# Out-projection weights in a hybrid decoder layer: load and split written as two pieces, each behind the softmax of a named attention step

## The chip, the cores and the metric

The kernel runs on one core of a Trainium2 chip. The metric is the time of one launch in microseconds (us) of the device, lower is better. Five engines work side by side: TensorE (PE in the profile, PEld for its weight loads), VectorE (DVE), ScalarE (ACT), GpSimd (POOL) and SyncE (SP), whose queue issues most of the DMA transfers. The built program holds one list of instructions for each engine; an instruction that waits holds back those that stand behind it in its list.

## The reference, cut to what matters

One decoder layer on 1024 tokens of width 1024, float32:

```
h = RMSNorm(x);  z = h @ W_in                      # one projection, columns split
A = dilated sliding-window attention(q, k, v)      # 8 heads x 64, then RMSNorm with attn_out_gain
R = RWKV-7 time mixing(z)                          # 8 heads x 64
x = x + RMSNorm(concat[A, R] @ W_out)              # W_out: 1024 x 1024
x = x + RMSNorm(relu(RMSNorm(x) @ W_up)^2 @ W_down)
```

The change concerns the preparation of `W_out`. The three branches of the attention are computed as one dense causal attention with a bias table (`stripT`), so that each softmax row is one exponential over its keys.

## The kernel before, in words

All large products are done as three products of rounded parts (`mm3`, lines 49 to 67): an operand `a` is split into a rounded `hi` and the rest `lo`, and `hi*hi + lo*hi + hi*lo` is summed in PSUM. So every weight block has to be split before TensorE can use it: ScalarE writes `hi`, VectorE subtracts it from the raw block and writes `lo`.

The program has these stages in time: input norm and transposes; a long stage in which the columns of `z` are projected slab by slab while the RWKV units are woven in (`drive`, up to about 447 us in the profiled execution); the attention (about 455 to 600 us); the out-projection with its norms ("mix", up to about 690 us); the up-projection and the down-projection of the feed-forward part.

**The attention** is written as 64 steps `m`. Step `m` stands for a pair of heads `p = m // 16`, a block of 128 queries `i` (in the order `TO` = 0, 4, 1, 5, 2, 6, 3, 7) and one head `h` of the pair; steps 1 and 2 are swapped. A step has these parts:

- `at_s`: TensorE forms the scores `pS` (two products per bank of 512 keys, 128*(i+1) keys in all) in PSUM banks of the tags `w` and `z`; VectorE adds the bias and takes the minimum (line 927, one instruction per bank, then a short read of the accumulator); ScalarE takes the exponential over the row (line 929).
- `at_t`: TensorE transposes the exponentials in blocks of 128 (`pT`, line 939) into the banks `a` and `c`, which exist once each; ScalarE copies the first four blocks out (line 941), VectorE the others (line 943).
- `at_v`: TensorE multiplies with the values (`po`); `at_vt` turns the values of the next pair (`vt`, again banks `a` and `c`).

The scores of step `m + 2` are written ahead of the transposes of step `m`, so TensorE runs two steps ahead of the softmax. The last slab of the projection, `z_av`, is woven into the start: its first half (24 products) and three parts of three products of its second half stand ahead of the first scores (`LEAD = 11` parts), and one part of three in each of the next steps. `z_av` uses the two banks `z`; its second half needs the bank that the eviction of the second half of `z_ak` frees (`evh_ak` on ScalarE, line 722, and `evl_ak` on VectorE, line 723).

**The out-projection weights** are eight blocks `k` of 128 x 1024. `load_wo(k)` (line 974) issues the load into a raw buffer (SyncE; tag `wr`, three buffers in rotation, which also hold `xr`, the residual input of the mix stage) and at once writes the split: two `hi` pieces of 512 columns on ScalarE and two `lo` pieces on VectorE. Blocks 4 to 7 meet the RWKV half of the mix and are split at lines 988 and 989; blocks 0 to 3 meet the attention half, carry the gain and are split at lines 983 and 984. The table `WOM` names the attention step at which the program text calls `load_wo`: 4 at step 17, 5 at 19, 6 at 33, 7 at 35, 0 at 37, then 1, 2, 3 at 49, 51, 53. Products with blocks 4 to 7 begin at step 40 in `r_ahead`, which fills gaps of the attention from step 39 on; products with blocks 0 to 3 begin after the last step.

**What sets the order.** TensorE keeps the order of the program text here (`manual_schedule`). ScalarE, VectorE and SyncE are ordered by the tile scheduler, which may put an instruction ahead of others when it thinks its inputs early enough; the attention's own instructions are written with a raised priority (`hi_pri`). `WOM` is thus only the place in the text. In the built program of before, the splits stand earlier than their steps.

Of the kernel before, what the change touches and what calls it, by code (L numbers as in the profile page):

```python
# [10 lines left out]
F32 = mybir.dt.float32  # L11
F32R = mybir.dt.float32r
I32 = mybir.dt.int32
AF = mybir.ActivationFunctionType
# [5 lines left out]
P = 128  # L20
S = 1024
D = 1024
# [20 lines left out]
def hybrid_kernel(tc, x, par, cst, strip, win, wup_lora, gup, gnwb, grow, wout, wup, wdown, out, dbg=None):  # L43
    nc = tc.nc
    PE, V, A, G = nc.tensor, nc.vector, nc.scalar, nc.gpsimd
    dbg = dbg or {}

    def mm(o, lhsT, rhs, start=True, stop=True):
        return PE.matmul(o, lhsT, rhs, start=start, stop=stop, skip_group_check=True)  # L49
# [16 lines left out]
    with (  # L66
# [801 lines left out]
        w2p = w2_ctx.__enter__()  # L868
# [9 lines left out]
        at, sx, pts, pos, aset = {}, {}, {}, {}, {0: hp}  # L878
# [14 lines left out]
        def at_raw(p):  # L893

            vT = at[p, "raw"] = hp[1].tile([P, S], F32, name=f"vT{p}", tag="raw", bufs=1)
            nc.sync.dma_start(vT, zs_d[20 + p])
# [14 lines left out]
        def at_s(p, i, h):  # L911

            QS, KH, KL = at[p]
            w = P * (i + 1)
            if (p, "den") not in at:
                at[p, "den"] = sm.tile([P, 8, 2], F32, name=f"den{p}", tag="den")
                at[p, "rden"] = sm.tile([P, 8, 2], F32, name=f"rden{p}", tag="rden")
            Sx = sx[p, i, h] = ap_.tile([P, S], F32, name=f"S{p}_{i}_{h}", tag="Sx", bufs=4)
            mn = sm.tile([P, 2], F32, name=f"mn{p}_{i}_{h}", tag="mn", bufs=4)
            nbk = 1 if w <= 512 else 2  # L920
            for k in range(nbk):
                lo, hi = 512 * k, min(w, 512 * k + 512)
                pS = ps.tile([P, 512], F32, name=f"pS{p}_{i}_{h}_{k}", tag="wz"[k] if p > 0 or TO.index(i) > 4 else "w")
                for q in range(2):
                    mm(pS[:, :hi - lo], QS[h][:, i * P:(i + 1) * P], (KH, KL)[q][h][:, lo:hi], q == 0, q == 1)
                so = S - w + lo
                V.tensor_tensor_reduce(Sx[:, lo:hi], pS[:, :hi - lo], stripT[:, so:so + hi - lo], 1.0,  # L927
                                       3e38 if k == 0 else mn[:, 0:1], OP.add, OP.min, accum_out=mn[:, k:k + 1])
            A.activation(Sx[:, :w], Sx[:, :w], AF.Exp, scale=-1.0, bias=mn[:, nbk - 1:nbk], accum_out=at[p, "den"][:, i, h:h + 1])  # L929

        def at_t(p, i, h):

            Sx = sx.pop((p, i, h))
            PT = pts[p, i, h] = ap_.tile([P, 8, P], F32, name=f"PT{p}_{i}_{h}", tag="PT", bufs=6)
            for k in range(1 if i < 4 else 2):
                nb_ = min(4, i + 1 - 4 * k)
                pt = ps.tile([P, 4, P], F32, name=f"pT{p}_{i}_{h}_{k}", tag="ac"[k], bufs=1)
                for j in range(nb_):
                    PE.transpose(pt[:, j], Sx[:, (4 * k + j) * P:(4 * k + j + 1) * P], ident)  # L939
                if k == 0:  # L940
                    A.activation(PT[:, 0:nb_], pt[:, 0:nb_], AF.Copy)  # L941
                else:
                    V.tensor_copy(PT[:, 4:4 + nb_], pt[:, 0:nb_])

        def at_v(p, i0):

            Vt = at[p, "v"]
            if i0 == 0:
                pos[p] = [ps.tile([P, 4, 2, 64], F32, name=f"po{p}_{qg}", tag="by"[qg], bufs=1) for qg in range(2)]
            for i in TO[i0:i0 + 2]:  # L950
                for h in range(2):
                    PT = pts.pop((p, i, h))
                    for j in range(i + 1):
                        mm_h(pos[p][i // 4][:, i % 4, h], PT[:, j], Vt[:, j, h * 64:h * 64 + 64], j == 0, j == i)
                if i0 == 6:
                    at_out(p, i // 4)
# [15 lines left out]

        WO = {}

        def load_wo(k, pool, tag):
            raw = stg.tile([P, D], F32, name=f"wo{k}", tag="wr", bufs=3)
            nc.sync.dma_start(raw, wout[k * P:(k + 1) * P, :])
            w = WO[k] = pool.tile([P, 2, D], F32R, name=f"WO{k}", tag=tag, bufs=4)
            if k < 4:
                ga = pr[:, PC_GATT + k:PC_GATT + k + 1]  # L980
                for n in range(2):
                    ns = slice(n * 512, n * 512 + 512)
                    A.activation(w[:, 0, ns], raw[:, ns], AF.Copy, scale=ga)
                    V.scalar_tensor_tensor(w[:, 1, ns], raw[:, ns], ga, w[:, 0, ns].bitcast(F32), OP.mult, OP.subtract)
            else:
                for n in range(2):
                    ns = slice(n * 512, n * 512 + 512)
                    A.activation(w[:, 0, ns], raw[:, ns], AF.Copy)
                    V.tensor_tensor(w[:, 1, ns], raw[:, ns], w[:, 0, ns].bitcast(F32), OP.subtract)

        M = {}
# [141 lines left out]
        ahead = {i: r_ahead(i, i == 2) for i in range(3)}  # L1133
        LEAD = 11
        RST = 8
        WOM = {17: 4, 19: 5, 33: 6, 35: 7, 37: 0, 49: 1, 51: 2, 53: 3}
        for _ in range(LEAD):
            next(rest, None)
        hi_pri = lambda: tc.high_priority(offset=PRI[3])
        def step(m):  # L1140
            m = {1: 2, 2: 1}.get(m, m)
            return m // 16, TO[m % 16 // 2], m % 2
# [5 lines left out]
        for m in range(64):  # L1148
            p, h = m // 16, m % 2
            i = m % 16 // 2  # L1150
            with hi_pri():
                if m + 2 < 64:
                    at_s(*step(m + 2))
                at_t(*step(m))
                if h == 1 and i % 2 == 0 and m > 1:
                    at_v(*((p, i - 2) if i else (p - 1, 6)))
                if h == 1 and i == 0:
                    at_vt(p)
                    if p < 3:
                        at_raw(p + 1)  # L1160
                if m == 17 or m == 33:
                    at_load(p + 1)
            if m < RST:
                next(rest, None)
            if m == RST:
                for _ in rest:
                    pass
                open_mix()
                with hi_pri():
                    at_load(1)  # L1170
            if m in WOM:
                k = WOM[m]
                load_wo(k, w2p if k > 3 else M["tp"], "w2" if k > 3 else "woA")
            for i_, m0 in ((0, 39), (1, 48)):
                if m0 <= m < m0 + 9:
                    next(ahead[i_], None)
            if m == 62:
                for g_ in (0, 1):
                    for _ in ahead[g_]:
                        pass  # L1180
                next(ahead[2])
# [5 lines left out]
        tp, tp_ctx = M["tp"], M["tc"]  # L1187
# [121 lines left out]
        raw = up_raw(4, "e2")  # L1309
        with tc.issue_after(ea.ins), tc.issue_after(ed.ins):  # L1310
# [3 lines left out]
            raw = up_raw(6, "e3")  # L1314
# [315 lines left out]
```

## Time and profile before

| | |
|---|---|
| three timed runs | 1301.68, 1307.09, 1309.77 us; median 1307.09 us |
| the profiled execution | 1310.87 us, of which the span from first to last instruction is 1308.7 us |
| PE busy / DVE / ACT / POOL | 97% / 69% / 48% / 3% of the span |
| mean granted TensorE clock | 0.991 of full |

The profile page gives busy times by engine, and a strip of 40 slices of 32.7 us. A view of windows gives busy time and granted clock in chosen stretches; the timeline lists instructions with their start, duration and the idle time ahead of them with what ended it. PE is busy nearly throughout, so the page alone says little; the slices that are not full are where time can be lost. Counted from 0, the attention lies in slices 14 to 18.

### The profile page before, as it was taken

The numbers are of one execution on the slowest core, as the hardware profiler recorded it, in microseconds if no ns is written. First come the engines' busy times: TensorE is split into PE (matmuls) and PEld (weight loads), VectorE is DVE, ScalarE is ACT, GpSimd is POOL, SyncE is SP. The second block draws the span as 40 slices with busy tenths as digits, with TensorE's granted clock in tenths as the row PEclk, the third lists the DMA queues.
The fourth block names the chain that finished last, engine by engine and source line by source line (L and its number), as shares of the span: only waits on it lengthen the run. The fifth ranks groups of instructions, "written<-read, shape, count | busy, mean of one in ns | idle before, by whom it ended". The sixth has DMA issues, their size and how long they took to land.

```text
span 1308.7 us, 23852 instructions
## 1 busy us (share of the span) xinstructions
PE 1264.9 (97%) x9488; PEld 1041.3 (80%) x9488; DVE 903.1 (69%) x1647; ACT 624.2 (48%) x1052; POOL 43.2 (3%) x61
## 2 busy tenths in 40 slices
PE   6999999999989889999999999999999999999997
PEld 5778888877767768888888888888888888888886
DVE  7877678533858657656879976776766775456884
ACT  7653433233545367666656544443444434443442
POOL 0000000000000000000000000000000002000221
PEclk9999999999999989999999999999999999999999
DMA  6456767966785665304434555435457984556642
GB/s 241 143 194 162 198 162 212 268 200 217 213 245 170 243 233 173 118 26 123 153 121 130 190 172 177 142 132 169 157 199 241 371 300 162 171 183 198 194 165 103
DMA packets 167870, 241.07 MB, mean 184 GB/s; under 512 B 56304, under 2 KB 93424, under 8 KB 167760
## 3 DMA queue, kind: packets, MB, share of 16 engines
q1 hardware_dynamic: 158256, 213.86, 50.7%
q10 hardware_dynamic: 8064, 20.98, 4.8%
q0 software_dynamic: 1440, 4.72, 1.0%
q8 instruction: 74, 1.21, 0.4%
q14 instruction: 36, 0.29, 0.1%
HBM read 162.16 MB, written 77.09 MB: 183 GB/s over the span
## 4 chain that ended last, share of the span: by engine, by line
PE 83%; DVE 7%; DMA 5%; ACT 3%; issue 1%; SPq 1%; DVEq 0%; ACTq 0%
PE X L49 12%; PE dX L49 12%; PE pm L49 7%; PE Z L49 7%; PE dZ L49 7%; PE z_v L49 3%; PE z_aq L49 3%; PE dY L49 3%; PE Y L49 3%; PE z_k L49 3%; PE z_r L49 2%; PE pS L49 2%; PE z_ak L49 2%; PE z_av L49 2%; PE po L49 2%; PE pT L939 2%
## 5 line engine op out<-in xcount | busy, mean ns | idle before, releaser
L49 PE MATMUL dX<-wow,wou 128*128 128x512 f32 x768 | 175.2, 389 | 0.4 <-DVE wow L1247 0.4
L49 PEld LDWEIGHTS dX<-wow,wou 128*128 128x128 f32 x768 | 144.0, 188 | 30.9 <-DVE wow L1247 1.1
L49 PE MATMUL dZ<-wow,wou 128*128 128x512 f32 x384 | 87.4, 389 | 0.0
L49 PEld LDWEIGHTS dZ<-wow,wou 128*128 128x128 f32 x384 | 72.1, 188 | 15.0
L1247 DVE TENSOR_TENSOR wou<-ur,wou 128x1024 fp32r<-128x1024 f32 x56 | 71.2, 1273 | 5.0 <-ACT wou L1246 4.9
L1246 ACT ACTIVATE wow<-wd 128x1024 fp32r<-128x1024 f32 x32 | 33.8, 1060 | 73.1 <-PE dX L49 25.8
L1247 DVE TENSOR_TENSOR wow<-TK,wow 128x1024 fp32r<-128x1024 f32 x24 | 30.6, 1274 | 50.0 <-ACT wow L1246 50.0
L1246 ACT ACTIVATE wou<-ur 128x1024 fp32r<-128x1024 f32 x56 | 58.5, 1047 | 13.7 <-DMA ur<-u_d 6.6
L1247 DVE TENSOR_TENSOR wow<-wd,wow 128x1024 fp32r<-128x1024 f32 x32 | 39.5, 1236 | 29.6 <-ACT wow L1246 29.3
L927 DVE CUSTOM_DVE_ANT_0 S<-pS,stripT 128x512 f32<-128x512 f32 (+3 forms) x64 | 37.6, 589 | 26.9 <-PE pS L49 24.0
L1246 ACT ACTIVATE wow<-TK 128x1024 fp32r<-128x1024 f32 x24 | 25.4, 1059 | 63.0 <-PE dX L49 32.5
L929 ACT ACTIVATE S<-S,mn 128x128 f32<-128x128 f32 (+7 forms) x64 | 49.3, 771 | 12.5 <-DVE mn L927 12.0
L1344 ACT ACTIVATE r<-u 128x512 f32<-128x512 f32 x48 | 30.1, 627 | 51.8 <-DVE u L1342 51.6
L49 PE MATMUL pm<-WO,mxr 128*128 128x512 f32 x192 | 49.1, 400 | 0.8 <-DVE mxr L1012 0.8
L49 PE MATMUL z_av<-hT,wh_av 128*128 128x512 f32 x128 | 47.3, 421 | 1.6 <-DVE evl_ak L723 1.6
L1552 POOL TENSOR_TENSOR E<-E,gpF 128x512 f32<-128x512 f32 x12 | 22.4, 1882 | 786.5 <-DMA xf<-x_d 626.4
L939 PE MATMUL pT<-cst,S 128*128 128x128 f32 x288 | 44.8, 281 | 3.0 <-ACT PT L941 1.8
L49 PE MATMUL pm<-WO,mxa 128*128 128x512 f32 x192 | 46.1, 395 | 0.2 <-ACT mxa L1011 0.2
L49 PE MATMUL Z<-HB,wo 128*128 128x512 f32 x192 | 46.1, 389 | 0.0
L49 PE MATMUL z_aq<-hT,wh_aq 128*128 128x512 f32 x128 | 44.5, 406 | 0.0
L49 PE MATMUL dY<-wow,wou 128*128 128x512 f32 x192 | 43.7, 389 | 0.0
L49 PE MATMUL z_ak<-hT,wh_ak 128*128 128x512 f32 x128 | 43.6, 402 | 0.0
(396 smaller groups left out, 3080.6 us busy)
## 6 DMA issues: line engine op xcount, KB each, us to landing
ur<-u_d SPq DMA_DIRECT2D x56, 512.0 KB, 4.4
u_d<-S SPq DMA_DIRECT2D x64, 256.0 KB, 2.2
wd<-in_wdown_dram SPq DMA_DIRECT2D x32, 512.0 KB, 4.5
u_d<-u SPq DMA_DIRECT2D x48, 256.0 KB, 2.3
TK<-in_wdown_dram SPq DMA_DIRECT2D x24, 512.0 KB, 6.0
wr_upa<-in_wup_dram SPq DMA_DIRECT2D x16, 512.0 KB, 3.7
wr_upb<-in_wup_dram SPq DMA_DIRECT2D x16, 512.0 KB, 4.1
x<-in_x_dram SPq DMA_DIRECT2D x8, 512.0 KB, 6.4
```

The source lines that it names most:

```text
L49: return PE.matmul(o, lhsT, rhs, start=start, stop=stop, skip_group_check=True)
L927: V.tensor_tensor_reduce(Sx[:, lo:hi], pS[:, :hi - lo], stripT[:, so:so + hi - lo], 1.0, 3e38 if k == 0 else mn[:, 0:1], OP.add, OP.min, a ...
L929: A.activation(Sx[:, :w], Sx[:, :w], AF.Exp, scale=-1.0, bias=mn[:, nbk - 1:nbk], accum_out=at[p, "den"][:, i, h:h + 1])
L939: PE.transpose(pt[:, j], Sx[:, (4 * k + j) * P:(4 * k + j + 1) * P], ident)
L1246: A.activation(w[:, 0, 0:n], raw, AF.Copy)
L1247: low = E.tensor_tensor(w[:, 1, 0:n], raw, w[:, 0, 0:n].bitcast(F32), OP.subtract)
L1344: A.activation(r, src, AF.Relu)
L1552: G.tensor_tensor(e, e, gn[n], OP.mult)
```

## The change

The exponential of a step is kept in `at["exp"]`. `load_wo` is cut in two: `load_wo(k)` allocates the raw buffer and issues the load, `split_wo(k)` makes the four pieces. The table is new: loads at steps 12, 16, 20, 24 (blocks 4 to 7) and 36, 40, 44, 48 (blocks 0 to 3), and each split four steps (`WOL`) after its load. Both calls stand in a block `with tc.issue_after(at["exp"].ins)`, which keeps each ScalarE instruction written in it behind the latest exponential, that of step `m + 2`, in ScalarE's order. The loads are on SyncE and get no such tie.

```
-            A.activation(Sx[:, :w], Sx[:, :w], AF.Exp, scale=-1.0, ...)
+            at["exp"] = A.activation(Sx[:, :w], Sx[:, :w], AF.Exp, scale=-1.0, ...)
...
-        def load_wo(k, pool, tag):
-            raw = stg.tile([P, D], F32, name=f"wo{k}", tag="wr", bufs=3)
-            nc.sync.dma_start(raw, wout[k * P:(k + 1) * P, :])
+        RAW = {}
+
+        def load_wo(k):
+            RAW[k] = stg.tile([P, D], F32, name=f"wo{k}", tag="wr", bufs=3)
+            nc.sync.dma_start(RAW[k], wout[k * P:(k + 1) * P, :])
+
+        def split_wo(k, pool, tag):
+            raw = RAW.pop(k)
             w = WO[k] = pool.tile([P, 2, D], F32R, name=f"WO{k}", tag=tag, bufs=4)
...
-        WOM = {17: 4, 19: 5, 33: 6, 35: 7, 37: 0, 49: 1, 51: 2, 53: 3}
+        WOM = {12: 4, 16: 5, 20: 6, 24: 7, 36: 0, 40: 1, 44: 2, 48: 3}
+        WOL = 4
...
-            if m in WOM:
-                k = WOM[m]
-                load_wo(k, w2p if k > 3 else M["tp"], "w2" if k > 3 else "woA")
+            with tc.issue_after(at["exp"].ins):
+                if m in WOM:
+                    load_wo(WOM[m])
+                if m - WOL in WOM:
+                    k = WOM[m - WOL]
+                    split_wo(k, w2p if k > 3 else M["tp"], "w2" if k > 3 else "woA")
```

The same instructions are issued, with the same shapes, and TensorE's order is the same word for word. What moves is the place of the pieces on ScalarE and VectorE, and of some loads on SyncE. Three places show it.

**ScalarE where the projection ends and the attention begins, before.** `WO` is a split block, `wo` its raw buffer (numbers tell the blocks apart), `evh_ak` and `ev_av` are evictions of the projection, `S` with `den` is an exponential:

```order
L722 ACTIVATE evh_ak_0_5205<-z_ak_0_5180 128x512
L724 DMA qk_d<-evh_ak_0_5205 128x512
L988 ACTIVATE WO_5894<-wo_5892 128x512 x2
L722 ACTIVATE evh_ak_1_5236<-z_ak_1_5211 128x512
L988 ACTIVATE WO_5935<-wo_5933 128x512
L724 DMA qk_d<-evh_ak_1_5236 128x512
L988 ACTIVATE WO_5935<-wo_5933 128x512
L988 ACTIVATE WO_6377<-wo_6375 128x512 x2
L988 ACTIVATE WO_6418<-wo_6416 128x512
L733 ACTIVATE ev_av_0_5293<-z_av_0_5268 128x512
L988 ACTIVATE WO_6418<-wo_6416 128x512
L739 DMA zs_d<-ev_av_0_5293 128x512
```

The same place now:

```order
L722 ACTIVATE evh_ak_0_5205<-z_ak_0_5180 128x512
L724 DMA qk_d<-evh_ak_0_5205 128x512
L722 ACTIVATE evh_ak_1_5236<-z_ak_1_5211 128x512
L724 DMA qk_d<-evh_ak_1_5236 128x512
L733 ACTIVATE ev_av_0_5293<-z_av_0_5268 128x512
L739 DMA zs_d<-ev_av_0_5293 128x512
L929 ACTIVATE S_0_0_5323,den_5321<-S_0_0_5323,mn_0_0_5324 128x128
L929 ACTIVATE S_4_0_5330,den_5321<-S_4_0_5330,mn_4_0_5331 128x640
```

All eight `hi` pieces of blocks 4 to 7 stood here among the evictions, ahead of the first exponential; now none does. VectorE's eight `lo` pieces (line 989) likewise stood around `evl_ak` ahead of the first line 927, and are gone from there. The eight `hi` pieces of blocks 0 to 3 (line 983) stood in steps 8 to 16 of the attention, and are gone from there too.

**ScalarE at steps 18 to 24, in the second head pair, now.** `PT` is a copy of transposed exponentials, `sqa` a square for the norm, `Vt` a copy of turned values:

```order
L941 ACTIVATE PT_0_1_5808<-pT_0_1_0_5809 128x128
L993 ACTIVATE WO_5792<-wo_5673 128x512
L929 ACTIVATE S_4_1_5797,den_5733<-S_4_1_5797,mn_4_1_5798 128x640
L969 ACTIVATE sqa_0_5832<-ao_0_5829 128x512
L993 ACTIVATE WO_5792<-wo_5673 128x512
L909 ACTIVATE Vt_5874<-vt_0_5875 128x512
```

The two `hi` pieces of block 4 now stand singly between exponentials and copies; those of blocks 5, 6 and 7 follow in the same way up to step 32, and those of blocks 0 to 3 stand singly or in pairs between steps 40 and 55, where `r_ahead` runs.

**SyncE's queue in the second head pair, now.** `qs`, `kh` and `kl` are the attention's inputs of a head pair (`kh_0_5893` to `kl_1_5891` those of pair 2, `kh_0_6381` and after those of pair 3), `a_d` a store of attention output, `vT` the raw values of the next pair:

```order
L889 DMA kh_1_5890<-qk_d 128x1x1024
L889 DMA kl_1_5891<-qk_d 128x1x1024
L966 DMA a_d<-ao_0_5829 128x4x128
L979 DMA wo_6053<-in_wout_dram 128x1024
L966 DMA a_d<-ao_1_5868 128x4x128
L896 DMA vT_5887<-zs_d 128x1024
L979 DMA wo_6439<-in_wout_dram 128x1024
L889 DMA kh_0_6381<-qk_d 128x1x1024
```

The loads of blocks 4, 5 and 6 stand where they stood, in the RWKV stage, since the three raw buffers are free there. The loads of block 7 (`wo_6053`) and of block 0 (`wo_6439`), which stood ahead of the second pair's inputs, now stand here, each waiting for the raw buffer of the third block before it; those of blocks 1, 2 and 3 and the three `xr` loads follow later, in that order.

More of the change, by code (lines that the diff above doesn't have):

```diff
@@ L928, in at_s @@
                                        3e38 if k == 0 else mn[:, 0:1], OP.add, OP.min, accum_out=mn[:, k:k + 1])
-            A.activation(Sx[:, :w], Sx[:, :w], AF.Exp, scale=-1.0, bias=mn[:, nbk - 1:nbk], accum_out=at[p, "den"][:, i, h:h + 1])
+            at["exp"] = A.activation(Sx[:, :w], Sx[:, :w], AF.Exp, scale=-1.0, bias=mn[:, nbk - 1:nbk], accum_out=at[p, "den"][:, i, h:h + 1])
         def at_t(p, i, h):
```

## The prediction

> **What bounds the kernel now.** I read the strip of 40 slices first, to see where TensorE is not the bound.
>
> ```profile
> PE   6999999999989889999999999999999999999997
> PEclk9999999999999989999999999999999999999999
> ```
>
> Apart from the first and the last slice PE is below 9 only in slices 11, 13 and 14 (counted from 0), and only in slice 14 is the granted clock low. Slice 14 is 458 to 491 us, the start of the attention. So I cut that stretch into windows (columns: PE, PEld, DVE, ACT, POOL busy us with counts, granted clock, DMA share, GB/s).
>
> ```profile
> 453.00:457.80 4.80, 3.12 (x14) 2.21 (x13) 4.06 (x7) 2.81 (x6) 0.54 (x1) 1.00 0.61 161
> 457.80:462.20 4.40, 0.00 (x0) 0.00 (x0) 1.61 (x5) 1.74 (x3) 0.00 (x0) 0.93 0.99 399
> 462.20:466.00 3.80, 3.77 (x12) 3.17 (x13) 1.31 (x7) 1.96 (x7) 0.00 (x0) 0.50 0.51 164
> 466.00:470.00 4.00, 3.53 (x17) 3.03 (x17) 1.50 (x6) 2.00 (x4) 0.00 (x0) 0.50 0.00 0
> 470.00:471.90 1.90, 1.90 (x8) 1.62 (x7) 0.78 (x2) 0.19 (x1) 0.00 (x0) 0.51 0.59 151
> 471.90:475.00 3.10, 3.10 (x21) 2.77 (x20) 1.28 (x6) 1.85 (x7) 0.00 (x0) 1.00 0.21 82
> 479.00:495.00 16.00, 14.65 (x204) 11.99 (x206) 14.62 (x37) 15.54 (x31) 0.00 (x0) 1.00 0.95 352
> 495.00:541.00 46.00, 44.52 (x644) 38.50 (x641) 32.36 (x101) 34.19 (x82) 0.00 (x0) 1.00 0.54 176
> 545.00:600.00 55.00, 55.00 (x767) 48.10 (x765) 31.86 (x89) 35.87 (x77) 0.00 (x0) 1.00 0.14 40
> ```
>
> PE stands still for 4.4 us and then works 9.7 us at half clock. From 479 to 495 us ACT and DVE are nearly full and PE is not. From 545 us on PE is full. The timeline tells why PE stood still:
>
> ```profile
> 442.24 0.60 ACT L722 ACTIVATE evh_ak<-z_ak 128x512 fp32r<-128x512 f32 x1 [4.44 <-PE z_ak L49]
> 452.09 1.15 ACT L988 ACTIVATE WO<-wo 128x512 fp32r<-128x512 f32 x2 [9.26 <-DMA vT<-zs_d]
> 452.69 0.39 PE L49 MATMUL z_av<-hT,wh_av 128*128 128x512 f32 x1
> 454.71 0.50 PE L49 MATMUL z_av<-hT,wh_av 128*128 128x512 f32 x1 [1.63 <-DVE evl_ak L723]
> 456.90 0.22 PE L49 MATMUL pS<-kh,qs 128*128 128x128 f32 x1
> 458.64 0.63 ACT L988 ACTIVATE WO<-wo 128x512 fp32r<-128x512 f32 x1 [2.83 <-DMA wo<-in_wout_dram]
> 461.89 0.28 DVE L927 CUSTOM_DVE_ANT_0 S<-pS,stripT 128x128 f32<-128x128 f32 x1
> 462.23 0.48 PE L49 MATMUL pS<-kh,qs 128*128 128x128 f32 x1 [4.49 <-DMA wo<-in_wout_dram]
> ```
>
> ACT reaches the first weight piece at 442.8 us and waits 9.26 us for memory that it may write. Behind it stands the second eviction of `z_ak`, so `z_av` starts its second half late. Then ACT waits 2.83 us for the load of block 7, whose buffer came free only when block 4 was split. DVE takes its pieces in turn, and the first reduction of the scores comes at 461.89 us, though its scores were there by 457.3.
>
> **The change, first term: the start of the attention.** Neither ACT nor DVE has a weight piece there now, so I replay PE's unchanged order with the durations of the trace at full clock. These rows carry it beside those above:
>
> ```profile
> 462.10 0.69 DVE L927 CUSTOM_DVE_ANT_0 S<-pS,stripT 128x512 f32<-128x512 f32 x1
> 463.36 0.83 ACT L929 ACTIVATE S<-S,mn 128x640 f32<-128x640 f32 x1 [0.65 <-DVE mn L927]
> 464.18 0.39 ACT L929 ACTIVATE S<-S,mn 128x128 f32<-128x128 f32 x1
> 464.57 0.25 ACT L941 ACTIVATE PT<-pT 128x128 f32<-128x128 f32 x1
> 467.13 0.60 ACT L941 ACTIVATE PT<-pT 128x512 f32<-128x512 f32 x1 [2.31 <-PE pT L939]
> 468.94 0.60 ACT L909 ACTIVATE Vt<-vt 128x512 f32<-128x512 f32 x1 [0.40 <-PE vt L905]
> 472.34 0.28 PE L49 MATMUL pS<-kh,qs 128*128 128x256 f32 x1
> 472.58 0.71 PE L939 MATMUL pT<-cst,S 128*128 128x128 f32 x5
> 502.58 1.09 PE L905 MATMUL vt<-cst,vT 128*128 128x128 f32 x8
> ```
>
> 1. `z_av`'s second half follows its first directly: 452.69 + 0.23 (the spacing of such products) = 452.9 instead of 454.7, 1.8 us earlier. Nine products later the first scores start at 455.0, and their reduction at 455.35 instead of 461.89: 6.5 us earlier.
> 2. The second reduction needs the next product, done at 455.8: 455.87 to 456.56 (0.69). The third ends at 457.0, its exponential runs 457.05 to 457.9, the next 0.39 to 458.26, then the copy of the first transposes (0.25) to 458.5. That copy frees bank `a`, so the transposes of step 1 start at 458.56. After 0.63 us they can be copied: 459.2 to 459.8 (0.60).
> 3. That frees bank `a` for `vt`: 459.85, and PE is past it 0.8 us later, at 460.7. Three products of `z_av` (0.7), one pair of scores (0.25), one transpose (0.1) and three more products (0.7) bring PE to the scores that stood at 472.34: at 462.4.
>
> So PE gets there 9.9 us earlier; from that point it worked at full rate before too (471.9 to 475), and the lead is kept. It is made of 1.8 us for `evl_ak`, 4.4 us of standstill and some 3.7 us, mostly the half clock.
>
> The half clock is a term that I take from the windows: 9.2 us of work at 0.50 is 4.6 us at full clock, and the replay needs 6.4 us for it with its waits for bank `a`, so 9.7 - 6.4 = 3.3. The Trainium skill (TensorE: Matmul & The Clock Gate, Part 1: The HAM clock gate) says that the clock goes to half after one idle window of about 3.4 us and back after about 3.4 us of sustained work. By that the half rate would have ended some 3.4 us after 462.2, the loss would be 1.7 us and this sum smaller by 1.6. The trace shows 9.7 us, with PE at 3.53 of 4 us busy in its midst, and it decides.
>
> **Second term: steps 8 to 16.** The eight pieces of blocks 0 to 3 leave the stretch in which ACT was full. PE's work from the scores of block 2 to the first scores of the next pair is the same in pair 0 and in pair 1; only in pair 0 do pieces stand in it:
>
> ```profile
> 478.18 0.44 PE L49 MATMUL pS<-kh,qs 128*128 128x384 f32 x1
> 495.16 0.33 PE L49 MATMUL pS<-kh,qs 128*128 128x128 f32 x1
> 509.67 0.44 PE L49 MATMUL pS<-kh,qs 128*128 128x384 f32 x1
> 524.51 0.33 PE L49 MATMUL pS<-kh,qs 128*128 128x128 f32 x1
> ```
>
> 16.98 - 14.84 = 2.1 us for eight pairs of pieces. That is also the price of a pair, 0.27 us of PE where pieces stand densely.
>
> **Third term: the pieces where they now stand.**
>
> ```profile
> L988 ACT ACTIVATE WO<-wo x8: 615/618/632, 452.1 to 460.6; 128x512 fp32r<-128x512 f32 x8
> L989 DVE TENSOR_TENSOR WO<-wo,WO x8: 684/688/693, 452.8 to 461.3; 128x512 fp32r<-128x512 f32 x8
> L983 ACT ACTIVATE WO<-wo,par x8: 708/712/714, 478.8 to 490.8; 128x512 fp32r<-128x512 f32 x8
> L984 DVE SCALAR_TENSOR_TENSOR WO<-wo,par,WO x8: 746/748/753, 479.5 to 493.9; 128x512 fp32r<-128x512 f32 x8
> ```
>
> Blocks 4 to 7 go into steps 18 to 32, within 495 to 541 us. ACT there goes from 34.2 to 39.1 of 46 us, DVE from 32.4 to 37.9, PE has 44.5: still the most loaded. A piece can cost nothing (its step's exponential has two steps of scores ahead of it) or, packed as in pair 0, 0.27 us. Eight pairs: 0 to 2.1 us. They stand half as densely, so I take 1.0. Blocks 0 to 3 go to steps 40 to 55, where `r_ahead` keeps PE at 55.0 of 55 us: ACT goes from 35.9 to 41.6, DVE to 37.8. Again 0 to 2.1; with that cover I take 0.4, and without it 2.1. A gain is excluded in both, since work is only added. Loads cost nothing: blocks 4 to 6 are loaded where they were, long before, and the load of block 7 or 0 waits for a buffer freed some eight steps before its split. Behind it on SyncE stand a store of attention output and `vT`, wanted at step 33, and the inputs of pair 3, wanted at step 46.
>
> **Sum.** 9.9 + 2.1 - 1.0 - 0.4 = 10.6 us: 1310.87 becomes 1300.3 in the profiled execution. That one stands 3.8 us above the median; from the median it is 1307.1 - 10.6 = **1296.5 us**. The stages after the attention should only move forward, as PE is full in them. The ends of the third term give a gain of 7.8 to 12.0, so 1295.1 to 1299.3.
>
> **Rivals.**
>
> *The clock falls all the same.* In the replay PE still waits briefly for banks, at most 0.5 to 0.8 us at a time. The clock also fell after a wait shorter than 4.4 us:
>
> ```profile
> 269.76 1.44 PE L49 MATMUL qu<-X,N 64*64 64x64 f32 x64 [2.61 <-DVE X L527]
> 272.00:274.00 2.00, 2.00 (x14) 1.68 (x13) 0.76 (x2) 0.00 (x0) 0.00 (x0) 0.53 0.00 0
> ```
>
> The 3.3 us of half clock would stay: 1299.8. Against it stands the window 479 to 495, with 1.35 us of short waits and clock 1.00. The same page of the Trainium skill (A second HAM failure mode: psum-queue depth-cycling) says that brief idling between groups that cycle through PSUM banks can make the clock swing; that would be this rival.
>
> *The wait is handed on.* The first reduction writes memory of the same release as the first weight piece and may inherit its wait. That ended at 452.09, and the reduction is due at 455.35: 3.2 us of cover. Were the standstill and the half clock to stay, 1.8 + 2.1 - 1.4 = 2.5 is left: 1304.6.
>
> *Slower: the pieces join the softmax chain.* Each piece then delays its exponential by its whole length, and PE's lead of two steps does not absorb it: 8 x (0.618 + 0.688) + 8 x (0.712 + 0.748) = 22.1 us against a gain of 12.0, and waits of that kind bring one stretch of half clock, 3.3: 1320.5. It decides from the point where ACT has more work than PE between 495 and 541, which needs 10.3 us more on ACT; it gets 4.9.
>
> *It does not do what it says.* The tie holds ScalarE only, and three loads did not move. Were the pieces early as before, 1307. The order shows them late.
>
> **How the numbers follow.** Forecast 0.76, clock 0.10, handed on 0.08, slower 0.04, nothing 0.02. The three runs lie from 5.4 below to 2.7 above their median, so I put some 5 us below the best end of the mechanism and as much above its worst: 1290 to 1304, which also holds the clock rival. About 1% (13 us) is what a measurement of this kernel can tell from no change. The forecast of 0.8% lies under it; with the spread of the runs it passes 13 us about 3 times in 10: faster 0.22, same 0.75, slower 0.03.
>
> **What would show it.** Right: no ACT wait of 9 us at 442 us; the first line 927 near 455.4; full clock in slice 14; 9 to 10 us of lead when the scores of block 2 start (478.18 before), 11 to 12 at the first scores of pair 1, and 10 to 11 at 600 us. Wrong: half clock between 455 and 475; a wait of the first reduction on a DMA beyond 455; pair 1 longer than 16 us between its two markers; PE below 54 of 55 us in the `r_ahead` stretch.

## The result, and the profile after

The changed kernel takes 1296.09 us in the median of six runs (1294.06 to 1300.73), the kernel before 1306.55 (six runs beside it, 1301.68 to 1309.77): ratio 0.993, 95% interval 0.9904 to 0.9955. A later set of eleven runs of the changed kernel gave 1297.54 beside 1304.11, ratio 0.9946 (0.9922 to 0.9969). So it is faster by 0.5 to 0.7%: both intervals lie below 1, though the gain is smaller than the 1% that the prediction took for what a measurement of this kernel can tell. The profiled execution took 1298.98 us, span 1297.2, clock 0.996.

The strip of 40 slices of the changed kernel, to be read beside the one of before: slices 11, 13 and 14 now read 9 (90% or more), and no slice has a low clock.

```profile
PE   7999999999999999999999999999999999999997
PEclk9999999999999999999999999999999999999999
```

Windows of the changed kernel (columns as before: PE, PEld, DVE, ACT, POOL, granted clock, DMA share, GB/s) over the start of the attention, pair 1 and the `r_ahead` stretch:

```profile
450.00:455.00 5.00, 4.52 (x23) 3.56 (x22) 1.53 (x7) 1.25 (x4) 0.00 (x0) 1.00 0.49 172
455.00:460.00 5.00, 4.33 (x28) 3.61 (x27) 2.22 (x9) 3.38 (x10) 0.00 (x0) 1.00 0.04 12
460.00:463.00 3.00, 3.00 (x21) 2.65 (x20) 1.42 (x6) 1.88 (x7) 0.00 (x0) 1.00 0.43 162
...
484.00:530.00 46.00, 42.87 (x623) 36.56 (x623) 35.34 (x105) 36.29 (x85) 0.00 (x0) 1.00 0.55 193
545.00:590.00 45.00, 45.00 (x658) 39.59 (x657) 30.91 (x81) 32.45 (x70) 0.00 (x0) 1.00 0.28 89
```

The standstill and the half clock are gone: 1.00 everywhere. But the 46 us around pair 1 hold 42.87 us of PE, where the 46 us of before (495 to 541) held 44.52. The two windows do not begin at the same place of the pair; counted from its first scores, they hold 42.60 and 44.52.

To compare the two traces, an origin is needed that the change can't have moved. The first product of `z_av` (here its first one in the last slab, at 447.48 us of before) is one: up to it the instructions that compute on each engine, and SyncE's transfers, come in the same order in both traces. Timeline rows of before, that origin and the last stretch of 96 `po` products in the attention:

```profile
447.48 0.39 PE L49 MATMUL z_av<-hT,wh_av 128*128 128x512 f32 x1
...
597.16 3.02 PE L49 MATMUL po<-Vt,PT 128*64 128x64 f32 x96
```

And of the changed kernel, with the rows that answer to those of the prediction between:

```profile
445.23 0.39 PE L49 MATMUL z_av<-hT,wh_av 128*128 128x512 f32 x1
...
453.08 0.29 DVE L927 CUSTOM_DVE_ANT_0 S<-pS,stripT 128x128 f32<-128x128 f32 x1 [6.33 <-PE pS L49]
...
460.37 0.28 PE L49 MATMUL pS<-kh,qs 128*128 128x256 f32 x1
...
466.20 0.45 PE L49 MATMUL pS<-kh,qs 128*128 128x384 f32 x1
...
481.91 0.33 PE L49 MATMUL pS<-kh,qs 128*128 128x128 f32 x1
...
497.81 0.44 PE L49 MATMUL pS<-kh,qs 128*128 128x384 f32 x1
...
513.60 0.33 PE L49 MATMUL pS<-kh,qs 128*128 128x128 f32 x1
...
586.21 3.02 PE L49 MATMUL po<-Vt,PT 128*64 128x64 f32 x96
```

The origin itself lies 447.48 - 445.23 = 2.25 us earlier, which the change can't have done. From it to the last `po` the attention took 597.16 - 447.48 = 149.68 us and now takes 140.98: **8.70 us less**. The rest of the 11.5 us between the two spans is those 2.25 us and 0.55 us behind the attention.

By stretches, in us, for all profiled executions of this study. "Start" is from the origin to the second 128x256 scores (472.34 before), "to block 2" from there to the first 128x384 scores (478.18 before), "0b" on to the first scores of pair 1; "1a" and "1b" are the halves of pair 1, parted by its 128x384 scores; then pairs 2 and 3, and their sum.

| kernel | origin at | start | to block 2 | 0b | 1a | 1b | 2 | 3 | attention |
|---|---|---|---|---|---|---|---|---|---|
| before | 447.48 | 24.86 | 5.84 | 16.98 | 14.51 | 14.84 | 35.04 | 37.61 | 149.68 |
| changed | 445.23 | 15.14 | 5.83 | 15.71 | 15.90 | 15.79 | 35.10 | 37.51 | 140.98 |
| changed, again | 440.33 | 15.15 | 5.84 | 15.71 | 15.89 | 15.78 | 35.09 | 37.50 | 140.96 |
| no tie | 442.39 | 24.89 | 5.83 | 16.99 | 14.50 | 14.84 | 35.02 | 37.61 | 149.68 |
| before + filler | 442.23 | 21.50 | 5.84 | 17.00 | 14.50 | 14.84 | 35.03 | 37.59 | 146.30 |
| tie alone | 440.97 | 15.15 | 5.84 | 15.72 | 16.54 | 14.84 | 37.88 | 38.55 | 144.52 |
| without splits 4 to 6 | 439.87 | 15.15 | 5.84 | 15.71 | 14.50 | 14.84 | 35.71 | 37.52 | 139.27 |
| block 4 later | 440.37 | 15.14 | 5.85 | 15.71 | 14.49 | 15.77 | 35.09 | 37.53 | 139.58 |
| 4 to 7 later | 438.42 | 15.15 | 5.84 | 15.71 | 14.50 | 15.92 | 35.03 | 37.52 | 139.67 |
| 4 to 6 earlier | 448.70 | 15.15 | 5.84 | 16.79 | 14.43 | 14.84 | 35.75 | 37.52 | 140.32 |
| exponential behind copy | 448.08 | 15.14 | 5.83 | 14.84 | 15.89 | 15.80 | 35.11 | 37.54 | 140.15 |
| both steps | 444.11 | 15.15 | 5.84 | 14.84 | 14.51 | 15.77 | 35.07 | 37.51 | 138.69 |
| both, tied in pair 1 too | 445.56 | 15.15 | 5.84 | 14.84 | 14.64 | 15.75 | 35.02 | 37.52 | 138.76 |
| both, block 5 in pair 2 | 443.13 | 15.15 | 5.83 | 14.84 | 14.51 | 15.37 | 35.11 | 37.52 | 138.33 |

Two things are to be seen before any experiment. The stretches are the program's: where two kernels have the same order in a stretch, it agrees within some 0.03 us ("changed" and "changed, again" in every column). The origin is not: it lies anywhere between 438.4 and 448.7 us, so a single total tells nothing about a change of 2 us, and the stretches are what the experiments are read by. And the gain has one large giver, the start (24.86 - 15.14 = 9.72), and one place that gives back: pair 1 went from 29.35 to 31.69 us.

Where pair 1 loses, in the timeline of the changed kernel:

```profile
489.32 1.10 PE L905 MATMUL vt<-cst,vT 128*128 128x128 f32 x8
...
490.41 0.68 DVE L994 TENSOR_TENSOR WO<-wo,WO 128x512 fp32r<-128x512 f32 x1
...
491.01 0.68 DVE L964 TENSOR_TENSOR ao<-po,rden 128x512 f32<-128x512 f32 x1
491.61 0.41 DVE L927 CUSTOM_DVE_ANT_0 S<-pS,stripT 128x256 f32<-128x256 f32 x1
...
491.95 0.69 DVE L907 COPY Vt<-vt 128x512 f32<-128x512 f32 x1
492.78 0.30 PE L939 MATMUL pT<-cst,S 128*128 128x128 f32 x1 [1.30 <-DVE Vt L907]
...
501.80 0.55 PE L939 MATMUL pT<-cst,S 128*128 128x128 f32 x3 [0.52 <-ACT PT L941]
```

`vt` is written into the banks `a` and `c`, which the next transposes need. The copy that frees `c` (line 907, on DVE) stands behind a `lo` piece of block 4, the scaling of an attention output (`ao`) and a reduction, and PE waits 1.30 us for it. Further on PE waits 0.52 us for a copy on ACT; an exponential stands right ahead of that copy, and a piece of block 5 ahead of the exponential.

### The profile page after: what moved, and what is told of

Same layout as the page of the kernel before. It is cut to its first block, busy times and chain, and to the rows that moved or that the text cites. A ratio compares the mean times of both kernels' runs of the same rounds, so it can differ in the third digit from the quotient of the medians.

```text
span 1297.2 us, 23850 instructions
## 1 busy us (share of the span) xinstructions
PE 1260.0 (97%) x9488; PEld 1038.8 (80%) x9488; DVE 902.1 (70%) x1647; ACT 623.2 (48%) x1052; POOL 43.2 (3%) x61
## 4 chain that ended last, share of the span: by engine, by line
PE 84%; DVE 6%; ACT 5%; DMA 3%; issue 1%; SPq 0%; DVEq 0%; ACTq 0%
PE X L49 12%; PE dX L49 12%; PE pm L49 7%; PE Z L49 7%; PE dZ L49 7%; PE z_ak L49 4%; PE z_v L49 3%; PE dY L49 3%; PE z_av L49 3%; PE z_aq L49 3%; PE Y L49 3%; PE z_r L49 2%; PE O L49 2%; PE pT L939 2%; PE pS L49 2%; PE po L49 2%
## 5 line engine op out<-in xcount | busy, mean ns | idle before, releaser
L49 PEld LDWEIGHTS dZ<-wow,wou 128*128 128x128 f32 x384 | 72.1, 188 | 14.9
L1255 ACT ACTIVATE wou<-ur 128x1024 fp32r<-128x1024 f32 x56 | 58.5, 1048 | 14.9 <-DMA ur<-u_d 7.6
```

The source lines that it names most:

```text
L1255: A.activation(w[:, 0, 0:n], raw, AF.Copy)
```

## The experiments

The theories were: the gain is the standstill and the half clock at the start, and follows from ScalarE's order alone; and the loss in pair 1 belongs to the places at which pieces stand. The rivals are in each expectation. Expectations speak of "pair 0, second half" for 0b.

**No tie.**

```
-            with tc.issue_after(at["exp"].ins):
+            if True:
                 if m in WOM:
```

> The changed kernel without the tie to the exponentials; the two pieces and the new table stay. ScalarE's order is then that of the kernel before: the pieces of blocks 4 to 7 among the last evictions of the projection, those of blocks 0 to 3 in steps 8 to 16. Theory (the place of the pieces on ScalarE is the whole change): 1305 to 1309, the ScalarE wait of 9 us at 442 us and the half clock in slice 14 are back, first line-927 reduction 14 to 15 us behind the first half of z_av instead of 7.9. Rival (two pieces and table are enough): 1294 to 1299 with the profile of the changed kernel.

Measured: 1305.56 us (ten runs), ratio to before 0.9995 (0.997 to 1.0019). Two rows of its timeline:

```profile
446.83 1.15 ACT L993 ACTIVATE WO<-wo 128x512 fp32r<-128x512 f32 x2 [9.09 <-DMA vT<-zs_d]
...
456.61 0.28 DVE L927 CUSTOM_DVE_ANT_0 S<-pS,stripT 128x128 f32<-128x128 f32 x1
```

The 9 us wait is back, the first reduction comes 456.61 - 442.39 = 14.22 us behind the origin, and every stretch of the table is that of before. Cutting the load in two and the new table do nothing without the tie: the theory holds.

**Before, with filler products in the standstill.** It parts the standstill from the half clock.

```
+                if (p, i, h, k) == (0, 4, 0, 1):
+                    fill = ps.tile([P, 512], F32, name="fill", tag="c", bufs=1)
+                    for f_ in range(18):
+                        mm(fill, QS[h][:, 0:P], KH[h][:, 0:512], True, True)
                 for q in range(2):
                     mm(pS[:, :hi - lo], ...)
```

> The kernel before, with 18 added products of 128x512 (operands of the attention, result unused) written on TensorE between the second scores of the attention (block 4, first bank) and the third ones, so that TensorE works where it stood still for 4.4 us; every wait of ScalarE and VectorE stays as it was. Theory (the half clock is a cost of its own): the granted clock stays at 1.00 from 455 to 475 us, and the time from the first line-927 reduction to the 128x256 scores behind it (10.45 us before, 7.29 after the change) falls to 7.0 to 7.7 us, so some 3 us earlier at these scores than in the kernel before. Rival (in this stretch TensorE is held by ScalarE and VectorE whatever its clock): the clock stays at 1.00 and the time stays at 9.4 us or more. Third way: the clock falls all the same, and the time stays at 10.4.

Measured (one execution, 1301.93 us), windows over the standstill and the stretch that ran at half clock before:

```profile
452.40:456.70 4.30, 4.19 (x19) 3.14 (x17) 1.28 (x2) 1.75 (x3) 0.00 (x0) 1.00 1.00 399
456.70:460.80 4.10, 3.11 (x17) 2.37 (x17) 2.79 (x14) 2.38 (x8) 0.00 (x0) 1.00 0.53 176
460.80:464.00 3.20, 2.97 (x20) 2.69 (x21) 1.17 (x4) 2.11 (x6) 0.00 (x0) 1.00 0.29 74
```

The clock stays at 1.00, with ScalarE and VectorE waiting as before. The first reduction is at 456.72, the 128x256 scores behind it at 463.73: 7.01 us against 10.45. The start is shorter by 24.86 - 21.50 = 3.36 us, and that is the price of the half clock by itself. The other 21.50 - 15.14 = 6.36 us of the start are the standstill and the late `evl_ak`. The Trainium skill (TensorE: Matmul & The Clock Gate, Part 1: The HAM clock gate) has full rate return after about 3.4 us of sustained work, which would have priced the half clock at 1.7 us, an estimate; the run gives twice that. Elsewhere in the trace of before the page's time holds: the clock is 0.50 from 270.47 to 273.88 us, with PE busy throughout, and 1.00 behind. Here PE had short waits in between (3.53 of 4 us busy); whether these held the clock down was not tried.

**The tie alone.** Old table, split at the step of the load.

```
-        WOM = {12: 4, 16: 5, 20: 6, 24: 7, 36: 0, 40: 1, 44: 2, 48: 3}
-        WOL = 4
+        WOM = {17: 4, 19: 5, 33: 6, 35: 7, 37: 0, 49: 1, 51: 2, 53: 3}
+        WOL = 0
```

> The changed kernel with the old table (17, 19, 33, 35, 37, 49, 51, 53) and load and split at the same step, so tied but not two pieces. The start of the attention is then that of the changed kernel (first line-927 reduction 7.9 us behind the first half of z_av, clock 1.00). Theory (the tie alone brings the gain; what the separate load adds is only cover for late loads): pair 0 as in the changed kernel; blocks 4 and 5 stand in pair 1 and 6 and 7 in pair 2, so pair 1 costs about 1.2 us instead of 2.3 and pair 2 about 1; in all 1295 to 1298. Rival (the load must be four steps ahead): ScalarE waits 2 us or more for a raw block at one of the eight splits, with the softmax behind it, and the time is 1300 to 1306.

Measured: 1301.68 us (ten runs; one of them took 2520 us, from a cause that is not known, and is left out of the ratio), ratio to before 0.9975 (0.9948 to 1.0002). The start is fully that of the changed kernel, so the tie brings the gain. The sizes were wrong: pair 1 costs 2.0 us, pair 2 2.8 and pair 3 0.9 more than before, in place of about 1.2 and 1. The rival isn't it either: no piece on ScalarE waits for a load. Its timeline shows what does it:

```profile
485.19 0.69 DVE L994 TENSOR_TENSOR WO<-wo,WO 128x512 fp32r<-128x512 f32 x1 [0.96 <-ACT WO L993]
...
487.00 0.68 DVE L994 TENSOR_TENSOR WO<-wo,WO 128x512 fp32r<-128x512 f32 x1
...
488.53 0.68 DVE L907 COPY Vt<-vt 128x512 f32<-128x512 f32 x1
489.36 0.30 PE L939 MATMUL pT<-cst,S 128*128 128x128 f32 x1 [1.97 <-DVE Vt L907]
...
528.17 0.87 PE L939 MATMUL pT<-cst,S 128*128 128x128 f32 x6 [0.94 <-ACT PT L941]
```

Both `lo` pieces of block 4 now stand between the start of `vt` (485.08 to 486.18 us) and the copy that frees its bank, among other work of DVE, and PE waits 1.97 us instead of 1.30. Block 5 follows behind this copy and costs nothing: 1a has lost 16.54 - 14.51 = 2.03, little more than that wait, and 1b is 14.84. The first half of pair 2, with blocks 6 and 7, repeats it with 16.55 us, and behind it PE waits 0.94 us for a copy of transposes, with an exponential and a piece of block 0 ahead of it on ScalarE. So the table matters, though not for the loads: it sets which copies the pieces stand ahead of.

**Without the splits of blocks 4 to 6.**

```
-                if m - WOL in WOM:
+                if m - WOL in WOM and WOM[m - WOL] in (4, 5, 6):
+                    RAW.pop(WOM[m - WOL])
+                elif m - WOL in WOM:
```

> The changed kernel without the splits of blocks 4, 5 and 6 (their loads stay; the products that use these blocks take the split of block 7), so less work is done. Theory (the pieces of blocks 4 to 6 cost what pair 1 lost): the half from the first scores of pair 1 to its 128x384 scores goes from 15.90 to 14.4 to 14.7 us, the half from there to the first scores of pair 2 from 15.79 to 14.8 to 15.3, and at the first scores of pair 2 the lead is 1.7 to 2.4 us larger than in the changed kernel. Rival (the loss in pair 1 has another cause, such as the earlier start of the pair, whose inputs or stores now come late): both halves stay within 0.4 us of 15.90 and 15.79.

The kernel of this run leaves out three of the eight splits, so it is not the layer any more; it serves for its time alone.

Measured (one execution, 1293.48 us): 1a is 14.50 and 1b 14.84, the values of before to 0.01 us. All the loss of pair 1 is these pieces; that the pair begins earlier costs nothing. The DVE copy, for comparison:

```profile
483.98 1.09 PE L905 MATMUL vt<-cst,vT 128*128 128x128 f32 x8
...
485.29 0.68 DVE L907 COPY Vt<-vt 128x512 f32<-128x512 f32 x1
...
508.50 1.09 PE L939 MATMUL pT<-cst,S 128*128 128x128 f32 x8 [1.08 <-ACT PT L941]
```

It starts 1.31 us behind `vt`; in the changed kernel it was 491.95 - 489.32 = 2.63. The 1.32 us between them are the wait of 1.30. They are not the length of the two pieces, though it is close to it (0.62 and 0.68 us). DVE's order in the two traces parts them: 0.38 us are a sum of squares on DVE (line 970) that starts later because ScalarE's square, which it reads, stands behind a `hi` piece; 0.60 us are the `lo` piece; and 0.34 us are a reduction of scores (491.61 above), which the built order now has ahead of the copy and which stands behind it in the run without the pieces. The last row is a surprise of the same kind: with blocks 4 to 6 gone, the scheduler put both halves of block 7 together ahead of the last copies of pair 1, and pair 2 became 0.6 us longer.

**Block 4 later.** One number of the table: its split at step 19 instead of 16.

> The changed kernel with one number changed: block 4 is split at step 19 instead of 16, so that its pieces stand behind the copies of the turned values of pair 1 instead of ahead of them; all else is at its place. In the changed kernel the first half of pair 1 (its first scores to its 128x384 scores) takes 15.90 us, the second half 15.79. Theory (what costs is a piece ahead of the copies that free the two transpose banks, not the number of pieces): first half 14.5 to 15.0, second half 15.6 to 16.2, 0.6 to 1.4 us won at the first scores of pair 2. Rival (each pair of pieces costs about 0.3 us wherever it stands in a pair): first half 15.5 or more, and nothing won.

Measured (one execution, 1293.69 us): 1a 14.49, 1b 15.77; 1.43 us won in pair 1, at the upper end of what was expected. All eight pairs of pieces are still there, and the three `hi` and two `lo` pieces that now stand in 1a behind the `Vt` copy are free. The same two rows as above, and the wait in 1b that stays:

```profile
484.48 1.09 PE L905 MATMUL vt<-cst,vT 128*128 128x128 f32 x8
...
485.78 0.68 DVE L907 COPY Vt<-vt 128x512 f32<-128x512 f32 x1
...
495.50 0.55 PE L939 MATMUL pT<-cst,S 128*128 128x128 f32 x3 [0.51 <-ACT PT L941]
```

1.30 us again. The place is what costs, not the count; the rival with one price for each pair of pieces is out.

**Blocks 4 to 7 later, and 4 to 6 earlier.** Splits at steps 22, 24, 26, 28; and splits at 8, 10, 12 with loads at 2, 4, 6.

```
-        WOL = 4
+        WOS = {22: 4, 24: 5, 26: 6, 28: 7, 40: 0, 44: 1, 48: 2, 52: 3}
...
-                if m - WOL in WOM:
-                    k = WOM[m - WOL]
+                if m in WOS:
+                    k = WOS[m]
```

> The changed kernel with blocks 4 to 7 split at steps 22, 24, 26 and 28 instead of 16, 20, 24 and 28: all eight pairs of pieces then stand behind the turned values' copies, twice as densely, in the second half of pair 1. Theory (place, not density): first half of pair 1 14.5, second half 15.6 to 16.2 (14.84 without a piece, and eight pairs of pieces cost 1.27 in the second half of pair 0), so 0.9 to 1.6 us earlier than the changed kernel at the first scores of pair 2. Rival (density, 0.27 us for each pair of pieces, as the prediction had it): second half 17.0, 0.2 us won. Other rival (a piece costs its time on ScalarE, 0.62): second half 19 and 2 us lost.

> The changed kernel with blocks 4, 5 and 6 split at steps 8, 10 and 12 (loaded at 2, 4 and 6); block 7 stays at 28. Theory (the second half of pair 0 takes 15.71 us without a piece, and the eight pairs that stood there before cost the rest of 16.98): second half of pair 0 16.5 to 17.0, pair 1 14.5 and 14.8, so 1.0 to 1.6 us earlier than the changed kernel at the first scores of pair 2. Block 7's pieces then come as two in a row ahead of the last transposes of pair 1, as in the run without blocks 4 to 6, and the first half of pair 2 takes 15.2 instead of 14.57. Rival (the pieces cost the same anywhere): 2.3 us in pair 0, nothing won.

Measured (one execution each, 1292.35 and 1305.34 us, with origins at 438.42 and 448.70): the later splits give 14.50 and 15.92, so pieces packed into 1b cost 1.08 us, where the changed kernel's in all of pair 1 cost 2.34. The earlier ones give 16.79 in 0b, 1.08 us for five pairs and the start of the sixth, and 14.43 and 14.84 in pair 1; block 7 then costs 0.65 in pair 2, as foreseen. So in these stretches a pair of pieces costs 0.15 to 0.22 us (seven pairs in 1b, five in 0b), and far more ahead of the copies of `vt`. In both kernels the gain up to the first scores of pair 2 lies in the range of the theory, and the rivals are out.

**The exponential behind the copy.** 0b takes 15.71 us in the changed kernel although no piece stands in it, and the same work takes 14.84 in pair 1. ScalarE's order differs. In the changed kernel's timeline (exponentials are line 929, copies of transposes line 941):

```profile
467.57 0.62 ACT L929 ACTIVATE S<-S,mn 128x384 f32<-128x384 f32 x1 [0.66 <-DVE mn L927]
468.18 0.57 ACT L941 ACTIVATE PT<-pT 128x512 f32<-128x512 f32 x1
468.81 0.88 PE L939 MATMUL pT<-cst,S 128*128 128x128 f32 x6 [0.63 <-ACT PT L941]
```

ScalarE runs the exponential first, which has two steps of time, and the copy that PE waits for second. The edit for steps 4 to 13 (`ex` issues the exponential of step m + 2, `at["cp"]` is the copy of step m):

```
                 at_t(*step(m))
+                if 4 <= m < 14:
+                    with tc.issue_after(at["cp"].ins):
+                        ex()
```

> The changed kernel with one thing more: in steps 4 to 13 the exponential of step m + 2 is written behind the copy of the transposes of step m and tied to it, so that ScalarE's order in pair 0 is that of pair 1 (copy first, exponential second). Theory (the second half of pair 0 takes 15.71 us against 14.84 in pair 1, without any weight piece, because in pair 0 ScalarE runs the exponentials ahead of the copies that free the transpose bank): 14.8 to 15.0, so 0.7 to 0.9 us earlier from the first scores of pair 1 on. Rival (pair 0 is slower for another reason, such as the last parts of the projection that stand ahead of it): 15.5 or more. Pair 1 and all behind it as in the changed kernel.

Measured (one execution, 1301.98 us): 0b is 14.84, all else as in the changed kernel. Its timeline at the same place (the edit shifts line numbers by one or two), now the copy first and no wait of PE:

```profile
470.14 0.60 ACT L943 ACTIVATE PT<-pT 128x512 f32<-128x512 f32 x1 [0.65 <-PE pT L941]
470.63 0.61 ACT L930 ACTIVATE S<-S,mn 128x384 f32<-128x384 f32 x1
```

So 0.87 us of the 2.14 between 0b and 1b of the kernel before were ScalarE's order, and only 1.27 the pieces.

**Three that put the steps together,** beside the changed kernel itself.

> The changed kernel itself once more, beside the next two. If the durations of its stretches belong to the program and not to a run, then from the first product of z_av: first line-927 reduction 7.85 us, second half of pair 0 15.71, pair 1 15.90 and 15.79, and the whole attention up to the last products of 48 blocks and more (96 instructions) 141.0 us, each within 0.1. The start of z_av itself lay anywhere from 438 to 449 us in the runs so far, so the total should spread by several us: 1290 to 1300, some 9 us below the kernel before.

> The changed kernel with the two single steps that won time: block 4 split at step 19, and in steps 4 to 13 the exponential tied behind the copy of the transposes. Theory (the two losses are independent): second half of pair 0 14.84 us, pair 1 14.5 and 15.8, attention 138.7 us, 2.3 us less than the changed kernel; time 1288 to 1298. Rival (the won time is lost again further on, since TensorE is full from pair 2 on or the inputs come late): attention 140 us or more.

> As the run before, but the exponential is tied behind the copy in pair 1 too (steps 4 to 13 and 19 to 30). In the changed kernel a piece of block 5 stands there between two exponentials and the copy behind the second, and TensorE waits 0.16 and 0.52 us for two copies. Theory (a good part of what the pieces still cost in the second half of pair 1 is this order): that half 15.0 to 15.4 us instead of 15.8, attention 138.0 to 138.4. Rival (what is left there is the pieces' own time on ScalarE): 15.7 or more.

> As the run with both steps (block 4 at 19, exponential behind the copy in steps 4 to 13), but block 5 is split at step 35 instead of 20, so that its pieces stand in pair 2 where those of block 4 stand in pair 1, behind the copies of the turned values; blocks 6 and 7 stay at 24 and 28. Theory (the price is one of the place: three pieces at that place in pair 1 cost nothing, and of the 0.93 us that are left in the second half of pair 1 some 0.7 belong to block 5): second half of pair 1 14.9 to 15.2 us, pair 2 14.5 and 20.5, attention 137.8 to 138.2, about 3 us less than the changed kernel; time 1287 to 1297. Rival (TensorE is so full in pair 2 that a piece there costs as much): first half of pair 2 15.0 or more, attention 138.5 or more.

| kernel | median (runs) | ratio to before | 95% |
|---|---|---|---|
| changed, again | 1297.54 (11) | 0.9946 | 0.9922 to 0.9969 |
| both steps | 1294.85 (7) | 0.9922 | 0.9894 to 0.9950 |
| both, tied in pair 1 too | 1294.49 (7) | 0.9918 | 0.9888 to 0.9947 |
| both, block 5 in pair 2 | 1295.11 (6) | 0.9912 | 0.9885 to 0.9939 |

The changed kernel repeats itself by stretches; its median here lies 6.6 us below the kernel before, not some 9 as expected. Both steps add up: 138.69 us of attention, 138.7 expected. The tie in pair 1 failed: 15.75 in 1b, not 15.0 to 15.4. The wait moved to the other copying engine:

```profile
497.69 0.56 DVE L927 CUSTOM_DVE_ANT_0 S<-pS,stripT 128x384 f32<-128x384 f32 x1 [0.20 <-PE pS L49]
498.17 0.42 DVE L945 COPY PT<-pT 128x256 f32<-128x256 f32 x1
...
498.74 0.41 PE L941 MATMUL pT<-cst,S 128*128 128x128 f32 x2 [0.31 <-DVE PT L945]
```

DVE's half of the copies now stands behind a second reduction of scores, which itself waits 0.20 us for TensorE; with both steps alone the copy stood ahead of it (495.86 and 496.20 us there). So the built order of DVE changed with the tie on ScalarE, and the piece's own time, which the rival names, is not shown to be the cause. Block 5 in pair 2 is free there (first half of pair 2 14.58 us, against 14.55 with both steps alone), which the rival excluded, but 1b falls only to 15.37, not to 14.9 to 15.2, and the attention to 138.33. Most of the 0.53 us that are left in 1b over a half without pieces lies at block 6, whose `hi` pieces stand two in a row, here and in the changed kernel:

```profile
500.68 1.13 ACT L995 ACTIVATE WO<-wo 128x512 fp32r<-128x512 f32 x2
501.33 0.69 DVE L996 TENSOR_TENSOR WO<-wo,WO 128x512 fp32r<-128x512 f32 x1 [1.80 <-ACT WO L995]
501.72 0.58 ACT L943 ACTIVATE PT<-pT 128x512 f32<-128x512 f32 x1
501.94 0.68 DVE L927 CUSTOM_DVE_ANT_0 S<-pS,stripT 128x512 f32<-128x512 f32 x1
502.35 1.35 PE L941 MATMUL pT<-cst,S 128*128 128x128 f32 x7
```

Both its `hi` pieces stand ahead of a copy and one `lo` piece ahead of a reduction, and the seven transposes take 1.35 us, which took 0.98 in the run without blocks 4 to 6. All three are faster than before beyond their intervals, and their traces give 2.2 to 2.7 us less attention than the changed kernel; in the timed runs their intervals overlap with the changed kernel's, so that they are faster than it rests on the traces.

## Why the prediction was right, and where not

The time was right (1296.5 predicted, 1296.09 measured); the sum was 1.9 us too large. Against its 10.6 us stand 8.70 in the trace: the medians of the two sets, 10.5 and 6.6 us apart, lie about that value, and that the first of them met the forecast so closely is chance.

- **First term, 9.9: measured 9.72, right.** The replay put the first reduction 455.35 - 447.48 = 7.87 us behind the origin, and it came after 7.85. It put the 128x256 scores at 462.4, 14.92 behind, and they came after 15.14. The half clock in it, 3.3 by the windows, is 3.36 by the filler run.
- **Second term, 2.1: measured 1.27, the mechanism right and the size off.** The step took all that 0b had over 1b for the price of the pieces, since PE's work is the same in both. ScalarE's order isn't the same, and 0.87 us of the difference had nothing to do with weights (shown by the run with the exponential behind the copy). The price of a pair of pieces there was 0.16, not 0.27.
- **Third term, blocks 4 to 7, 1.0: measured 2.40 (2.34 in pair 1, 0.06 in pair 2), outside its bound of 2.1.** This is the step that failed. It read a price for each pair of pieces from where they had stood and scaled it by density. The runs show that the same eight pairs cost 1.1 or 2.4 by where they stand, and that 1.4 of it is one block of the four, ahead of the copies of `vt`. The listing of ScalarE's order ahead of the prediction even shows a piece of block 4 in the row before `Vt`; the banks `a` and `c` exist once each, so a delay there has no step of slack, and that could have been seen.
- **Third term, blocks 0 to 3, 0.4: measured none** (pairs 2 and 3: 72.65 before, 72.61 now). The loads cost nothing either, as argued. The cover isn't a property of the stretch alone: in the run with the tie alone, where these blocks stand at steps 37, 49, 51 and 53, the second half of pair 2 and pair 3 took 1.7 us longer than before together; the wait of 0.94 us behind a piece of block 0 is in it, and how much of the rest is theirs was not separated.
- **Rivals.** The clock didn't fall, though PE still waits for banks in the start (8.85 us busy of the 10 from 450 to 460). The first reduction inherited no wait. The pieces do join the softmax chain at a few places, but through the copies of the transposes rather than the exponentials, and by waits of 1.30 us at most in the changed kernel.
- **The tests named.** No 9 us wait, first reduction, clock in slice 14, PE full in the `r_ahead` stretch: all as said. The leads, less the 2.25 us ahead of the origin, were 9.73 at the scores of block 2 (9 to 10 said), 11.00 at pair 1 (11 to 12) and 8.70 at the end (10 to 11, missed). The test on pair 1, "longer than 16 us between its two markers", was too lax: 1b took 15.79 against 14.84, and the larger loss lay in 1a, which it didn't look at.

## What to carry to other kernels

A filler instruction on a copying engine is priced by what stands behind it: ahead of the only copy that frees a single-buffered bank the pieces of one block cost 1.4 us, a few steps later nothing, and an average price from another stretch says neither. It also moves its neighbours, since the scheduler orders them anew, so read the whole order around the wait before a piece is given the blame. When two stretches with the same work differ, compare the order of every engine in both before the difference is booked on the one thing that catches the eye. And fix an origin in the trace that the change can't reach: here stretches of 15 us could be compared to a few hundredths of a microsecond, while totals wandered by ten.

## What was not expected of the hardware

The half clock has a price of its own even in a stretch where PE waits for other engines: 18 filler products of no use won 3.36 us.

The origin of the attention lies between 438.4 and 448.7 us in fourteen executions, and the granted clock between 380 and 400 us is one thing that varies ahead of it. Of the kernel before (origin at 447.48):

```profile
380.00:400.00 20.00, 17.64 (x266) 14.33 (x262) 14.15 (x40) 8.09 (x14) 0.00 (x0) 0.83 0.71 224
```

And of the kernel with blocks 4 to 7 later (origin at 438.42):

```profile
380.00:400.00 20.00, 18.32 (x310) 14.84 (x312) 15.05 (x33) 12.69 (x22) 0.00 (x0) 1.00 0.79 215
```

Up to that point the two kernels have the same computing instructions in the same order. The record settles a part of what this does to the origin. In windows from 260 to 280 and from 340 to 437 us the clock is 1.00 in six of the fourteen executions, whose origins lie between 438.42 and 442.39 us (mean 440.4); in the other eight it is lower in one or both (down to 0.83 and to 0.95), and their origins lie between 442.23 and 448.70. The three latest origins, 447.48, 448.08 and 448.70, lost some 5 us to the clock in these windows (length times one less the clock), of the 7 to 8 us by which they lie behind that mean. What makes one execution fall to half clock there and another not wasn't tried, and the rest of the spread stays open; the spread is as large as the gain studied here.
